# Products that nobody reads in TensorE's waits, and two held low parts moved ahead of expert 0

## The chip, the cores and the metric

The kernel runs on one core of a Trainium2 chip. The metric is the device time of one execution in microseconds (us), the median of several runs; lower is better. In the trace the engines are PE (TensorE's matmuls; PEld are its weight loads), DVE (VectorE), ACT (ScalarE), POOL (GpSimd) and SP (SyncE, which here issues DMAs); a trailing q (SPq, PEq) marks an engine's own queue.

## The reference

One transformer block in float32 on a sequence of 1024 tokens of width 1024: sparse attention and gated linear attention side by side, a layer norm, a hierarchical mixture of 32 experts of which each token takes two, and a second layer norm. What matters for the change is the end:

```python
x = layer_norm(DN_ALPHA * x + gt1[:, None, :] * y, ln1_g[l], ln1_b[l])
h2 = modulate(x, sh2, sc2)
f = hier_moe(h2, w_router_group[l], ..., w_exp_down[l])
x = layer_norm(DN_ALPHA * x + gt2[:, None, :] * f, ln2_g[l], ln2_b[l])
```

In `hier_moe` the router takes the best of 4 groups, then the best 2 of the 8 experts in it; a token's result is the sum of `gate * ((silu(t @ w1) * (t @ w3)) @ w2)` over its two experts.

## The kernel before

Tokens are worked on in eight tiles of 128. float32 products of full precision are made of three fast ones: every operand is split into a high part (ScalarE copies it into the fast format) and a low part (VectorE or GpSimd subtracts the high part from the original), and `mm3` multiplies high by high, high by low and low by high.

**The tiles of the output projection and router.** A loop over tiles computes the output projection (`products`), the residual and first norm, the modulated second norm, the transposes of the tile (`transposed`), the router's products (`logits`, TensorE), the choice of group and experts (`choose`, VectorE), the place of every token among its expert's slots (`place`: two small bf16 products and VectorE work), the list of slots (`slots`, TensorE), the gate weights (`weigh`: VectorE, two exponentials of ScalarE, VectorE) and these weights ordered by slots (`slot_weights`: VectorE masks, TensorE products into `gps`). The last tile, 7, has an order of its own, written out by hand at the end (from L1622 on). Each engine takes its instructions in the order in which the text issues them (`manual_schedule`); an instruction that waits holds up those behind it on its engine.

In that stretch the first two thirds of expert 0's weights are also split (`split(..., hold=True)`): ScalarE makes four high parts, and the four low parts, each one subtraction of 128x1024 on VectorE, are put on a list `held`; `low_parts(n)` issues the next n of them. Before the change all four stand behind the copies of the slot weights (L1650, L1652): one behind each half of expert 0's transposed input (`expert_x`), then two more, then the count of overfull experts (`count_blocks`) and the low parts of expert 1.

**The experts.** A loop over 32 experts gathers each expert's tokens, transposes them (L1669), multiplies by the gate and up weights (`expert_up`, 24 products of 512 columns into `eph`), gates (`expert_act`: ScalarE at L1682, VectorE at L1683), transposes (L1689) and multiplies by the down weights; results are scattered to `dy`. Weights are loaded ahead into a ring of twelve buffers by SP (`fetch_next`).

**The last stage.** Two rows of `dy` per token are loaded, added, multiplied by `gt2`, added to the kept `xa`, normalized and stored. Its order is the string `LAST`: a letter for a step, a digit for the tile. a and b add the two rows (on TensorE, as products with the identity, for tiles 3 and 5, else on VectorE), g multiplies by `gt2` (L1857, VectorE), x and z add `xa` and the gated rows as products with the identity into a buffer `fps` of PSUM, of which there are four (L1851; tiles 0 and 7 do it on VectorE instead), m copies the sum from PSUM with its mean (L1864, ScalarE), v takes the variance (squares on ScalarE at L1870, then a root on GpSimd, L1871 and L1872), s and o scale and shift (L1875, L1882, VectorE), and o stores. x1 to x4 need no rows of `dy` and stand first; the first step of TensorE that needs such rows is z1.

Of the kernel before, what the change touches and what calls it, by code (L numbers as in the profile page):

```python
# [21 lines left out]
D = 1024  # L22
# [59 lines left out]


LAST = """
x1 x2 x3 x4 b0 g0 m0 b1 v0 g1 s0 z1 b2 m1 o0 v1 a3 g2 s1 z2 b4 b3 m2 o1 v2 a5 g4 g3 z4 s2 z3 m4 b6
o2 v4 b5 g6 m3 x5 s4 v3 g5 x6 o4 z5 s3 b7 z6 m5 o3 v5 g7 m6 s5 v6 m7 o5 v7 s6 s7 o6 o7
"""

# [70 lines left out]
def block_kernel(ctx, tc, A, out, dbg=None, stop=99):  # L159
# [1132 lines left out]
    GP.iota(pid, pattern=[[S, 2], [128, NT]], base=1, channel_multiplier=1, allow_small_or_imprecise_dtypes=True)  # L1292
    ones = rtp.tile([128, 128], BF, name="ones")
    GP.memset(ones, 1.0)
    gat = rtp.tile([128, 2, NT], F32, name="gat")
    exf = rtp.tile([128, 2, NT], F32, name="exf")
    psf = rtp.tile([128, 2, NT], F32, name="psf")
# [40 lines left out]
        V.tensor_scalar(M1, iota[:, :NE], exf[:, 0, t:t + 1], None, op0=OP.is_equal)  # L1338
        V.scalar_tensor_tensor(Mb[:, t], iota[:, :NE], exf[:, 1, t:t + 1], M1, op0=OP.is_equal, op1=OP.add)

    def weigh(t):

        L, g8, m8 = (rt[t].pop(n) for n in ("L", "g8", "m8"))
        ng_ = rtw.tile([128, 4], F32, name="rng")
        V.tensor_tensor(ng_[:, 0:1], m8[:, 1:2], m8[:, 0:1], op=OP.subtract)
        V.tensor_tensor(L[:, :4], L[:, :4], g8[:, 0:1].to_broadcast([128, 4]), op=OP.subtract)
        SC.activation(L[:, :4], L[:, :4], AF.Exp, accum_out=ng_[:, 1:2])
        SC.activation(ng_[:, 0:1], ng_[:, 0:1], AF.Exp)
        V.scalar_tensor_tensor(ng_[:, 2:3], ng_[:, 0:1], 1.0, ng_[:, 1:2], op0=OP.add, op1=OP.mult)
        V.reciprocal(gat[:, 0, t:t + 1], ng_[:, 2:3])  # L1350
        V.tensor_tensor(gat[:, 1, t:t + 1], gat[:, 0, t:t + 1], ng_[:, 0:1], op=OP.mult)

    def place(t):

# [202 lines left out]
    def low_parts(n):  # L1557
        for _ in range(min(n, len(held))):
            V.tensor_tensor(*held.pop(0), op=OP.subtract)  # L1559
# [67 lines left out]
    W[0, 0] = split(raws.pop((0, 0)), 0, hold=True)  # L1627
    z = fast_second(t)
    place(t - 2)
    transposed(t)  # L1630
    W[0, 1] = split(raws.pop((0, 1)), 1, hold=True)
    fetch_next(FE1)
# [6 lines left out]
    choose(t)  # L1639
    place(t)  # L1640
    slots(t)
    keep(t, z)
    slot_rows(tps, 0, NE, rtp)
    for i in range(NX):
        gather_x(xg[i], gidx[:, i:i + 1])
    for i in range(2):
        weigh(t - 1 + i)
    for i in range(3):
        slot_weights(t - 2 + i)
    V.tensor_copy(gsl[:, :NE], gps)  # L1650
    PE.matmul(pos[:, NT], ones, run[:, NT], start=True, stop=True, skip_group_check=True)
    V.tensor_copy(cnt, pos[:, NT])  # L1652
# [114 lines left out]
    with tc.tile_pool(name="ex", bufs=2) as ex, tc.tile_pool(name="epp", bufs=1, space=PSUM) as epp:  # L1767
        prev = []
        for X in expert_x(ex, epp, xg[0]):
            low_parts(1)  # L1770
        low_parts(2)
        gather_x(xg[0], gidx[:, NX:NX + 1])
        fetch_next(FE0)
        count_blocks()

        def down(e):
            return expert_down(ex, epp, W.pop((e, 2)), Hs)

        def scatter(y, e):
            sc_ = scatter_y(y, sidx[:, e:e + 1])  # L1780
            for p_ in prev:
                tc.declare_no_dep(sc_.ins, p_.ins, reason="rows of other slots")
            prev.append(sc_)

        for e in range(NE):
            fetch_next(3)
            more = e + 1 < NE
            ph = expert_up(epp, (W.pop((e, 0)), W.pop((e, 1))), X)
            if more:
                for i in range(2):  # L1790
                    W[e + 1, i] = split(raws.pop((e + 1, i)), i)
            sg = expert_act(es2, ph, gsl[:, e:e + 1])
            if more:
                *_, X = expert_x(ex, epp, xg[(e + 1) % NX])
                if e + 1 + NX < NE:
                    gather_x(xg[(e + 1) % NX], gidx[:, e + 1 + NX:e + 2 + NX])
            W[e, 2] = split(raws.pop((e, 2)), 2)
            sc_ = down(e - 1) if e > 0 else None
            Hs = expert_h(es2, epp, sg)
            if e > 0:  # L1800
                scatter(sc_, e - 1)
            if e == NE - 4:
                xa = []
                for _ in range(FX0):
                    load_xa(SY)
                gb, gt2 = (page(pe).rearrange("p (t n) -> p t n", t=2) for _ in range(2))
                for j, src in enumerate(("ln2_g", "ln2_b")):
                    SY.dma_start(gb[:, j], A[src][0:1].to_broadcast([128, D]))
                gt2 = gt2[:, 0]
                SY.dma_start(gt2, dada[3:4].to_broadcast([128, D]))  # L1810
        scatter(down(NE - 1), NE - 1)
# [24 lines left out]
    with tc.tile_pool(name="fin", bufs=NT) as fp, tc.tile_pool(name="fpp", bufs=4, space=PSUM) as fpp:  # L1836
# [5 lines left out]
        fs = {}  # L1842
        st = fp.tile([128, 4, NT], F32, name="fst", bufs=1)
        s_, m_, q_, r_ = (st[:, i] for i in range(4))
        def summed(t, j, x, first):

            if first:
                fs[t, j] = fpp.tile([128, D], F32, name="fps")
            for half in range(2):
                sl = slice(half * 512, half * 512 + 512)  # L1850
                PE.matmul(fs[t, j][:, sl], ident, x[:, sl], start=first, stop=not first)  # L1851

        def added(t):
            V.tensor_tensor(rr[t], rr[t], r2s[t], op=OP.add)
# [22 lines left out]
        def shift(t):  # L1877
# [10 lines left out]
            "g": gated,  # L1888
            "x": lambda t: summed(t, 1, xa[t], True),
            "z": lambda t: summed(t, 1, rr[t], False),  # L1890
            "m": mean, "v": variance, "s": scale, "o": shift,
        }
        with tc.manual_schedule(engines=ALL):
# [32 lines left out]
```

## Time and profile before

| | us |
|---|---|
| median of 3 runs | 1409.38 |
| lowest and highest run | 1406.3 and 1409.62 |
| profiled execution | 1403.06 |
| its span, first to last instruction | 1401.3 |
| TensorE busy | 1308.8 (93%) |
| VectorE busy | 1145.8 (82%) |
| ScalarE busy | 717.4 (51%) |
| GpSimd busy | 440.5 (31%) |
| mean granted clock of TensorE | 0.967 |

Times within the trace count from the first instruction. The span is cut into stages by what runs: projections and attention up to about 875, the tiles of the output projection and router up to about 1030, the experts up to about 1344, the last stage behind that. The granted clock is a share of 2.4 GHz, and the rows show it at one of two levels, 1.0 and 0.5 (1.2 GHz); a mean between them is a stretch with both.

In a row of the timeline stand start, duration, engine, line, operation, output and inputs by the program's names, partitions by elements, how many instructions are merged, and in brackets the idle time of the engine ahead of it with what ended it. The duration of a matmul is modelled and overlaps with the next one; starts of neighbours give the pace.

### The profile page before, as it was taken

The page shows a single profiled execution, that of the slowest core. Times are in us where ns is not written, and L with a number is a line of the kernel's source. Part 1 is how long each engine was busy: PE and PEld are TensorE (multiplying, and loading weights), DVE is VectorE, ACT ScalarE, POOL GpSimd, SP SyncE. Part 2 cuts the span into 40 slices and gives each one's busy share as a digit, 9 for nine tenths or more (in the row PEclk, how much of TensorE's full clock was granted, in tenths as well). Part 3 has the DMA queues.
Part 4 walks back from the last instruction along what each step waited for, and adds up shares of the span by engine and source line. Part 5 has one row for each costly group of instructions (what it writes and reads, how often), then busy time and mean ns, then how long its engine had stood idle before and what let it go on. Part 6 is the DMA issues. An engine that isn't in the chain of part 4 may idle for free. (4 is left out here: it accounts for less than half of the span.)

```text
span 1401.3 us, 21266 instructions
## 1 busy us (share of the span) xinstructions
PE 1308.8 (93%) x7535; PEld 1057.7 (75%) x7535; DVE 1145.8 (82%) x2137; ACT 717.4 (51%) x1306; POOL 440.5 (31%) x474
## 2 busy tenths in 40 slices
PE   4989999999999999998989999999779999999965
PEld 2568888887888788985557778999758888888832
DVE  5738888887988899974788749788889999999947
ACT  1546765444244321323665644222248888889824
POOL 2422123375237521232544425211212222222114
PEclk9999999999999999999999999999869999999987
DMA  8475422112211223103864458745469999999954
GB/s 285 158 210 183 138 78 76 43 56 73 72 61 39 74 87 106 61 31 122 318 230 138 137 152 261 273 168 209 151 214 374 372 381 371 373 348 363 375 224 177
DMA packets 133998, 264.91 MB, mean 189 GB/s; under 512 B 20736, under 2 KB 71224, under 8 KB 131840
## 3 DMA queue, kind: packets, MB, share of 16 engines
q1 hardware_dynamic: 122960, 245.40, 50.4%
q0 software_dynamic: 9216, 16.80, 3.2%
q8 instruction: 60, 0.98, 0.3%
q10 hardware_dynamic: 1712, 1.32, 0.3%
q14 instruction: 50, 0.41, 0.1%
HBM read 229.61 MB, written 50.62 MB: 200 GB/s over the span
## 5 line engine op out<-in xcount | busy, mean ns | idle before, releaser
L1554 DVE TENSOR_TENSOR elo<-pg,ehi 128x1024 fp32r<-128x1024 f32 x188 | 219.0, 1219 | 17.6 <-ACT ehi L1549 8.9
L181 PE MATMUL pj<-hTh,whi 128*128 128x512 f32 (+1 forms) x528 | 211.0, 400 | 0.0
L182 PE MATMUL pj<-hTl,whi 128*128 128x512 f32 (+1 forms) x528 | 207.1, 392 | 1.9 <-DVE hTl L307 1.2
L183 PE MATMUL pj<-hTh,wlo 128*128 128x512 f32 (+1 forms) x528 | 207.2, 392 | 0.1
L815 POOL TENSOR_TENSOR wlo<-raw,whi 128x512 fp32r<-128x512 f32 x84 | 114.5, 1378 | 289.0 <-ACT whi L814 268.8
L1549 ACT ACTIVATE ehi<-pg 128x1024 fp32r<-128x1024 f32 x192 | 190.1, 1075 | 1.0 <-PE eph L183 1.0
L517 DVE MATCH_REPLACE8 acc<-m,acc 128x1024 f32<-128x1024 f32 (+2 forms) x192 | 167.1, 878 | 0.0
L514 DVE MAX8 m<-acc 128x8 f32<-128x1024 f32 (+2 forms) x192 | 162.2, 881 | 0.0
L496 DVE SCALAR_TENSOR_TENSOR acc<-ixr,iwt,acc 128x128 f32<-128x128 f32 (+3 forms) x120 | 107.3, 933 | 23.9 <-ACT ixr L489 23.1
L181 PEld LDWEIGHTS pj<-hTh,whi 128*128 128x128 f32 (+1 forms) x528 | 98.6, 187 | 23.1 <-issue 1.7
L183 PEld LDWEIGHTS pj<-hTh,wlo 128*128 128x128 f32 (+1 forms) x528 | 98.5, 186 | 22.9 <-issue 0.6
L182 PEld LDWEIGHTS pj<-hTl,whi 128*128 128x128 f32 (+1 forms) x528 | 98.8, 187 | 22.2 <-DVE hTl L307 2.7
L181 PE MATMUL pj<-whi,hTh 128*128 128x256 f32 x384 | 111.8, 291 | 0.0
L182 PE MATMUL pj<-wlo,hTh 128*128 128x256 f32 x384 | 108.6, 283 | 0.0
L183 PE MATMUL pj<-whi,hTl 128*128 128x256 f32 x384 | 108.5, 283 | 0.0
L181 PE MATMUL eph<-ehi,xh 128*128 128x512 f32 x256 | 105.4, 412 | 0.0
L182 PE MATMUL eph<-elo,xh 128*128 128x512 f32 x256 | 102.8, 402 | 1.1 <-DVE elo L1559 1.1
L183 PE MATMUL eph<-ehi,xl 128*128 128x512 f32 x256 | 102.4, 400 | 0.0
L489 ACT ACTIVATE ixr<-ips 128x128 f32<-128x128 f32 (+7 forms) x128 | 80.7, 653 | 41.7 <-PE ips L487 32.9
L1573 POOL DMA_INDIRECT xg<-dh,gidx x32 | 34.2, 1070 | 161.4 <-PE etp L1669 139.9
L181 PEld LDWEIGHTS pj<-whi,hTh 128*128 128x128 f32 x384 | 73.4, 191 | 6.9 <-issue 5.5
L181 PE MATMUL yps<-whi,pg 128*128 128x256 f32 x256 | 76.0, 297 | 0.2 <-ACT pg L1234 0.2
(318 smaller groups left out, 3128.2 us busy)
## 6 DMA issues: line engine op xcount, KB each, us to landing
pg<-in_w_exp_gate_dram SPq DMA_DIRECT2D x64, 512.0 KB
pg<-in_w_exp_up_dram SPq DMA_DIRECT2D x64, 512.0 KB
pg<-in_w_exp_down_dram SPq DMA_DIRECT2D x32, 1024.0 KB
raw<-in_w_in_dram SPq DMA_DIRECT2D x20, 1024.0 KB
wada<-in_w_ada_dram SPq DMA_DIRECT2D x16, 1024.0 KB
dgate<-gate SPq DMA_DIRECT2D x48, 256.0 KB
gate<-dgate SPq DMA_DIRECT2D x48, 256.0 KB
wada<-in_w_ada_dram SPq DMA_DIRECT2D x16, 512.0 KB
```

Of the source, the lines that this page charges most:

```text
L181: PE.matmul(ps, ah, bh, start=first, stop=False)
L182: PE.matmul(ps, ah, bl, start=False, stop=False)
L183: PE.matmul(ps, al, bh, start=False, stop=last)
L489: SC.activation(r, ps, AF.Relu)
L496: V.scalar_tensor_tensor(acc[i], r, sc, acc[i], op0=OP.mult, op1=OP.add)
L514: V.max(m, acc[i])
L517: V.match_replace(acc[i], m, acc[i], -3.0e38)
L815: GP.tensor_tensor(lo[:, k:k + 2], raw[:, k:k + 2], hi[:, k:k + 2].bitcast(F32), op=OP.subtract)
L1549: SC.activation(h3, src, AF.Copy)
L1554: V.tensor_tensor(*args, op=OP.subtract)
L1573: GP.indirect_dma_start(out=x, out_offset=None, in_=dh2, in_offset=bass.IndirectOffsetOnAxis(ap=gi, axis=0), bounds_check=S - 1, oob_is_er ...
```

## The change

- A helper `busy(ps, n)` issues n products of the 128x128 bf16 matrix of ones with the same matrix, repeated to 512 columns, into a PSUM tile. Nothing reads the results.
- 20 of them are issued in the last tile behind `place(t - 2)` and ahead of `transposed(t)`, into a further buffer of the ring `yps`.
- 10 of them are issued behind `slots(t)`, ahead of the slot weights.
- In the last stage a new step w4 issues 28 of them between x3 and x4, into tile 4's own buffer `fps`, which x4 then overwrites.
- `weigh` is divided into two parts: up to the exponentials, and the rest. For the last two tiles both first parts are issued, then one held low part, then both second parts.
- Another held low part is issued behind `slot_weights` and ahead of the copy of `gps`. The two that stood behind expert 0's input are gone there.

```diff
@@ -82,7 +82,7 @@
 
 
 LAST = """
-x1 x2 x3 x4 b0 g0 m0 b1 v0 g1 s0 z1 b2 m1 o0 v1 a3 g2 s1 z2 b4 b3 m2 o1 v2 a5 g4 g3 z4 s2 z3 m4 b6
+x1 x2 x3 w4 x4 b0 g0 m0 b1 v0 g1 s0 z1 b2 m1 o0 v1 a3 g2 s1 z2 b4 b3 m2 o1 v2 a5 g4 g3 z4 s2 z3 m4 b6
 o2 v4 b5 g6 m3 x5 s4 v3 g5 x6 o4 z5 s3 b7 z6 m5 o3 v5 g7 m6 s5 v6 m7 o5 v7 s6 s7 o6 o7
 """
 
@@ -1292,6 +1292,11 @@
     GP.iota(pid, pattern=[[S, 2], [128, NT]], base=1, channel_multiplier=1, allow_small_or_imprecise_dtypes=True)
     ones = rtp.tile([128, 128], BF, name="ones")
     GP.memset(ones, 1.0)
+
+    def busy(ps, n):
+
+        for _ in range(n):
+            PE.matmul(ps, ones, ones[:, None, :].to_broadcast([128, 4, 128]), start=True, stop=True)
     gat = rtp.tile([128, 2, NT], F32, name="gat")
     exf = rtp.tile([128, 2, NT], F32, name="exf")
     psf = rtp.tile([128, 2, NT], F32, name="psf")
@@ -1338,17 +1343,20 @@
         V.tensor_scalar(M1, iota[:, :NE], exf[:, 0, t:t + 1], None, op0=OP.is_equal)
         V.scalar_tensor_tensor(Mb[:, t], iota[:, :NE], exf[:, 1, t:t + 1], M1, op0=OP.is_equal, op1=OP.add)
 
-    def weigh(t):
-
-        L, g8, m8 = (rt[t].pop(n) for n in ("L", "g8", "m8"))
-        ng_ = rtw.tile([128, 4], F32, name="rng")
-        V.tensor_tensor(ng_[:, 0:1], m8[:, 1:2], m8[:, 0:1], op=OP.subtract)
-        V.tensor_tensor(L[:, :4], L[:, :4], g8[:, 0:1].to_broadcast([128, 4]), op=OP.subtract)
-        SC.activation(L[:, :4], L[:, :4], AF.Exp, accum_out=ng_[:, 1:2])
-        SC.activation(ng_[:, 0:1], ng_[:, 0:1], AF.Exp)
-        V.scalar_tensor_tensor(ng_[:, 2:3], ng_[:, 0:1], 1.0, ng_[:, 1:2], op0=OP.add, op1=OP.mult)
-        V.reciprocal(gat[:, 0, t:t + 1], ng_[:, 2:3])
-        V.tensor_tensor(gat[:, 1, t:t + 1], gat[:, 0, t:t + 1], ng_[:, 0:1], op=OP.mult)
+    def weigh(t, parts=(0, 1)):
+
+        L, g8, m8 = (rt[t][n] for n in ("L", "g8", "m8"))
+        if 0 in parts:
+            ng_ = rt[t]["ng"] = rtw.tile([128, 4], F32, name="rng")
+            V.tensor_tensor(ng_[:, 0:1], m8[:, 1:2], m8[:, 0:1], op=OP.subtract)
+            V.tensor_tensor(L[:, :4], L[:, :4], g8[:, 0:1].to_broadcast([128, 4]), op=OP.subtract)
+            SC.activation(L[:, :4], L[:, :4], AF.Exp, accum_out=ng_[:, 1:2])
+            SC.activation(ng_[:, 0:1], ng_[:, 0:1], AF.Exp)
+        if 1 in parts:
+            ng_ = rt[t]["ng"]
+            V.scalar_tensor_tensor(ng_[:, 2:3], ng_[:, 0:1], 1.0, ng_[:, 1:2], op0=OP.add, op1=OP.mult)
+            V.reciprocal(gat[:, 0, t:t + 1], ng_[:, 2:3])
+            V.tensor_tensor(gat[:, 1, t:t + 1], gat[:, 0, t:t + 1], ng_[:, 0:1], op=OP.mult)
 
     def place(t):
 
@@ -1627,6 +1635,7 @@
     W[0, 0] = split(raws.pop((0, 0)), 0, hold=True)
     z = fast_second(t)
     place(t - 2)
+    busy(lpp.tile([128, 512], F32, name="yps", bufs=5), 20)
     transposed(t)
     W[0, 1] = split(raws.pop((0, 1)), 1, hold=True)
     fetch_next(FE1)
@@ -1639,14 +1648,19 @@
     choose(t)
     place(t)
     slots(t)
+    busy(lpp.tile([128, 512], F32, name="yps", bufs=5), 10)
     keep(t, z)
     slot_rows(tps, 0, NE, rtp)
     for i in range(NX):
         gather_x(xg[i], gidx[:, i:i + 1])
     for i in range(2):
-        weigh(t - 1 + i)
+        weigh(t - 1 + i, (0,))
+    low_parts(1)
+    for i in range(2):
+        weigh(t - 1 + i, (1,))
     for i in range(3):
         slot_weights(t - 2 + i)
+    low_parts(1)
     V.tensor_copy(gsl[:, :NE], gps)
     PE.matmul(pos[:, NT], ones, run[:, NT], start=True, stop=True, skip_group_check=True)
     V.tensor_copy(cnt, pos[:, NT])
@@ -1768,7 +1782,6 @@
         prev = []
         for X in expert_x(ex, epp, xg[0]):
             low_parts(1)
-        low_parts(2)
         gather_x(xg[0], gidx[:, NX:NX + 1])
         fetch_next(FE0)
         count_blocks()
@@ -1842,13 +1855,18 @@
         fs = {}
         st = fp.tile([128, 4, NT], F32, name="fst", bufs=1)
         s_, m_, q_, r_ = (st[:, i] for i in range(4))
+
+        def tile_of(t, j):
+            if (t, j) not in fs:
+                fs[t, j] = fpp.tile([128, D], F32, name="fps")
+            return fs[t, j]
+
         def summed(t, j, x, first):
 
-            if first:
-                fs[t, j] = fpp.tile([128, D], F32, name="fps")
+            ps = tile_of(t, j)
             for half in range(2):
                 sl = slice(half * 512, half * 512 + 512)
-                PE.matmul(fs[t, j][:, sl], ident, x[:, sl], start=first, stop=not first)
+                PE.matmul(ps[:, sl], ident, x[:, sl], start=first, stop=not first)
 
         def added(t):
             V.tensor_tensor(rr[t], rr[t], r2s[t], op=OP.add)
@@ -1888,6 +1906,7 @@
             "g": gated,
             "x": lambda t: summed(t, 1, xa[t], True),
             "z": lambda t: summed(t, 1, rr[t], False),
+            "w": lambda t: busy(tile_of(t, 1)[:, :512], 28),
             "m": mean, "v": variance, "s": scale, "o": shift,
         }
         with tc.manual_schedule(engines=ALL):
```

## Rows read from the trace of the kernel before

**Rows 1.** Windows of the span, busy time per engine; last columns: granted clock, DMA share, GB/s

```profile
965.00:970.00 5.00, 5.00 (x32) 5.00 (x32) 3.89 (x19) 0.39 (x3) 0.00 (x0) 0.66 0.38 151
...
1007.00:1010.00 3.00, 0.00 (x0) 0.00 (x0) 2.90 (x5) 0.00 (x0) 2.72 (x4) 0.50 0.77 313
...
1260.00:1270.00 10.00, 10.00 (x50) 8.22 (x49) 9.41 (x12) 8.40 (x12) 2.10 (x2) 1.00 0.97 372
...
1360.00:1365.00 5.00, 3.79 (x5) 1.19 (x5) 4.48 (x4) 1.26 (x3) 1.45 (x1) 0.50 1.03 414
```

**Rows 2.** Timeline, end of the last tile: start, duration, engine, line, idle and releaser

```profile
1006.45 0.18 PE L1356 MATMUL sums<-run,ones 128*128 128x32 bf16 x1
...
1012.52 1.94 PE L1519 MATMUL yps<-ident,lx 128*128 128x128 f32 x8 [5.89 <-DVE lx L1507]
...
1018.46 0.20 DVE L1322 TENSOR_TENSOR rL<-yps,br 128x40 f32<-128x40 f32 x1 [0.27 <-PE yps L1528]
```

**Rows 3.** Timeline, slots and slot weights, up to expert 0's first transposes

```profile
1022.33 0.61 PE L1374 MATMUL tps<-rE,rP 128*128 128x32 f32 x2 [0.94 <-DVE rP L1369]
...
1024.51 0.16 DVE L1349 SCALAR_TENSOR_TENSOR rng<-rng 128x1 f32<-128x1 f32 x1 [0.46 <-ACT rng L1348]
...
1026.13 1.34 DVE L1379 TENSOR_SCALAR rEg<-jp,exf,gat 128x32 f32<-128x32 f32 x6
...
1026.48 2.77 PE L1380 MATMUL gps<-rEg,rP 128*128 128x32 f32 x12 [3.54 <-DVE rEg L1379]
...
1029.29 0.19 DVE L1650 COPY gsl<-gps 128x32 f32<-128x32 f32 x1 [1.82 <-PE sums L1651]
...
1029.63 1.97 PE L1669 MATMUL etp<-ident,xg 128*128 128x128 f32 x8 [0.35 <-DVE cnt L1652]
```

**Rows 4.** Timeline, expert 0, VectorE and TensorE

```profile
1031.46 0.69 DVE L1671 TENSOR_TENSOR xl<-etp,xh 128x512 fp32r<-128x512 f32 x1 [1.89 <-ACT xh L1670]
...
1033.34 0.79 PE L182 MATMUL eph<-elo,xh 128*128 128x512 f32 x1 [1.06 <-DVE elo L1559]
...
1033.81 3.49 DVE L1559 TENSOR_TENSOR elo<-pg,ehi 128x1024 fp32r<-128x1024 f32 x3
...
1043.69 0.46 DVE L1683 SCALAR_TENSOR_TENSOR esg<-esg,gsl,eph 128x256 f32<-128x256 f32 x1
...
1044.20 0.44 PE L1689 MATMUL ehp<-ident,esg 128*128 128x128 f32 x2 [2.36 <-DVE esg L1683]
```

**Rows 5.** Timeline, 512-column products of expert 0, two at each clock

```profile
1034.36 0.63 PE L181 MATMUL eph<-ehi,xh 128*128 128x512 f32 x1
...
1037.35 0.58 PE L182 MATMUL eph<-elo,xh 128*128 128x512 f32 x1
...
1038.46 0.40 PE L183 MATMUL eph<-ehi,xl 128*128 128x512 f32 x1
...
1040.56 0.40 PE L183 MATMUL eph<-ehi,xl 128*128 128x512 f32 x1
```

**Rows 6.** Timeline, ScalarE in a later expert

```profile
1061.33 0.39 ACT L1682 ACTIVATE esg<-eph 128x256 f32<-128x256 f32 x1 [1.06 <-PE eph L183]
```

**Rows 7.** Timeline, last stage

```profile
1344.89 7.13 PE L1851 MATMUL fps<-pg,ident 128*128 128x512 f32 x16 [1.17 <-ACTq L1817]
...
1359.92 3.75 PE L1851 MATMUL fps<-fr,ident 128*128 128x512 f32 x4 [7.90 <-POOL fst L1871]
...
1363.71 1.02 ACT L1864 ACTIVATE fr<-fps 128x1024 f32<-128x1024 f32 x1 [4.57 <-PE fps L1851]
...
1366.36 1.28 DVE L1875 SCALAR_TENSOR_TENSOR fr<-fr,fst,pg 128x1024 f32<-128x1024 f32 x1 [1.89 <-ACT fj L1870]
...
1395.12 1.42 DVE L1882 SCALAR_TENSOR_TENSOR fr<-fr,fst,pg 128x512 f32<-128x512 f32 x2 [0.44 <-POOL fst L1872]
```

**Rows 8.** Groups of VectorE in 1352 to 1397: busy, mean ns; idle before, releasers

```profile
L1882 DVE SCALAR_TENSOR_TENSOR fr<-fr,fst,pg 128x1024 f32<-128x1024 f32 (+1 forms) x9 | 10.4, 1161 | 1.3 <-POOL fst L1872 1.3
...
L1875 DVE SCALAR_TENSOR_TENSOR fr<-fr,fst,pg 128x1024 f32<-128x1024 f32 x8 | 10.2, 1280 | 2.4 <-ACT fj L1870 2.4
```

## The prediction

> **What bounds the kernel now.** I began with the windows of the span, whose next-to-last columns are the granted clock and the DMA share. In the long run of experts TensorE is busy 10.00 us of each 10 at the full clock, while the loads hold the DMA engines at 0.97 [rows 1]; ScalarE waits for TensorE's product each time [rows 6]. There TensorE sets the pace, and nothing of the change lies there. Two other places stand at 0.50 of the clock, the lower level of 1.2 GHz instead of 2.4: the end of the last tile with the start of expert 0, and the head of the last stage [rows 1]. In both the clock fell while TensorE was waiting or had only short products.
>
> The timeline then shows who ends each wait. In the last tile it is VectorE: the transposes wait 5.89 us for the second norm [rows 2], the slot weights 3.54 us for the gate weights [rows 3]. VectorE itself is free for pieces of that stretch: 0.46 us ahead of a weight (once for each of two tiles), 1.82 us ahead of the copy of the slot weights, 1.89 us ahead of expert 0's first low part [rows 3, 4]. From then on it is full: it reaches the gating product of expert 0 at 1043.69, and TensorE stands 2.36 us for that [rows 4]. So VectorE, not TensorE, ends the start of the experts. In the last stage products wait 7.90 us for VectorE, then run at half clock (four in 3.75 us), and VectorE next waits 1.89 us for the chain behind them [rows 7].
>
> **The price of a product.** At half clock seven 512-column products start within 1037.35 - 1034.36 = 2.99 us, 0.427 us each; at the full clock nine within 1040.56 - 1038.46 = 2.10 us, 0.233 each [rows 5]. The trace has no bf16 product of 512 columns; its only bf16 ones have 32 [rows 2]. I take 0.233 and 0.427, the nearest in length. The upper end at the full clock is the last stage's float32 form, 7.13 / 16 = 0.446 per instruction [rows 7]. As an estimate, the Trainium skill's page "TensorE: Matmul & The Clock Gate", section "Wait — 56ns, not 53.3ns?", has 215.7 and 426.7 ns for a bf16 product of this length; by it the 28 take 6.0 us where I have 6.5, and the end of the kernel is the same, since both end inside the wait.
>
> **Part 1, 20 products ahead of the last transposes.** They follow the product that ends at 1006.63 and lie under the 5.89 us wait, until 1012.52 [rows 2]. At half clock all the way they end at 1006.63 + 8.5 = 1015.2, 2.7 us late; all at the full clock at 1011.3. In expert 0 it rose between 1037.35 and 1038.46, after dense products from 1033.34 [rows 4, 5]; if it rises as far into the fillers, nine or so cost 0.427 and eleven 0.233: 1006.63 + 3.8 + 2.6 = 1013.0, 0.5 us late. The eight transposes then need some 1.0 us instead of 1.94 [rows 2], so they end where they did. The next choice waits for the router's products only 0.27 us [rows 2]; that is the most to gain. I take -0.2, from -0.3 to +2.7, the lower end being the nearer by the price of rows 5.
>
> **Part 2, 10 products behind the last slots.** They start at 1022.9 [rows 3]. At half clock they end at 1027.2, 0.7 us after the slot weights could start at 1026.48; if the clock rises on the way, about 1026.8. The twelve slot-weight products then take about 1.6 us at the full clock instead of 2.77 [rows 3]: end 1028.8 instead of 1029.25. If it does not rise: 1030.0. I take -0.4, from -0.5 to +0.7.
>
> A rule speaks against both: TensorE's starts stand in program order in every row of the trace here. The Trainium skill, "TensorE: Matmul & The Clock Gate", section "Part 3: Packing small matmuls — row/col tiling", says that matmuls keep strict order, so a filler that outlasts its wait holds up the real product; the trace agrees. By that Parts 1 and 2 would cost up to 2.7 and 0.7; it is the rival C below.
>
> **Part 3, two low parts.** One is worth 3.49 / 3 = 1.16 us of VectorE [rows 4]. The first now stands between the halves of the weights; it fills the two waits of 0.46 us [rows 3] and delays the rest by 1.16 - 0.92 = 0.24. The two activations ahead of it are done before it ends, as both weights' first halves now go first. The second fills the 1.82 us ahead of the copy [rows 3] and costs nothing; without that cover it would cost 1.16. What they leave is VectorE's full stretch from 1031.46 to 1043.69: 12.23 - 2.3 = 9.9 us. Nothing else there falls: ScalarE's high parts of expert 1 lie ahead of their low parts by more than 2.3 us. TensorE no longer waits 1.06 us for a low part [rows 4], and its 24 products, started near 1030.6, end by 1038.6 even with eight at half clock, ahead of the gating product's new time. So VectorE still decides.
>
> Sum for the start of the experts: -2.3 for the low parts, +0.2 (the one's overhang, on the chain to the slot weights), -0.4 (slot weights), -0.2 (last tile): -2.7. Bounds: -1.6 where the clock stays low through the slot weights, -3.1 at best; one half-clock stretch in expert 1 may vanish as well, eight products at 0.427 - 0.233 = -1.6 [rows 5]. From there TensorE is full through all experts, so the shift goes to their end. The loads move too: they wait for buffers that the low parts and products free, so they are asked for earlier by as much.
>
> **Part 4, 28 products in the last stage.** Three of four sums ahead take 12 x 0.446 = 5.3 us from 1344.89; the 28 take 6.5, the fourth sum 1.8: 1358.5 [rows 7]. The waiting product starts at 1359.92 as before, since VectorE releases it; 1.4 us stay idle. At the full clock four instructions take 1.8 instead of 3.75 us, so the copy at 1363.71 comes at 1361.7, and the scaling at 1366.36 starts when its predecessor ends, 1364.5: -1.9. What is late next is VectorE itself, which is busy nearly all of the time from there: it waits 2.4 us in all for ScalarE's squares and 1.3 us for GpSimd's roots [rows 8]. TensorE's stretch behind the first product shortens as well, so the other waits for squares should go (2.4 - 1.89 = 0.5), and those for roots but the last one, of the last tile (1.3 - 0.44 = 0.9) [rows 7, 8], since a root then has its time while VectorE works on other tiles. That is -1.9 - 0.5 - 0.9 = -3.3, and the last shift starts near 1391.8 instead of 1395.12. Bounds: -1.9 (the first wait alone) and -3.7 (all of rows 8); -1.0 if the clock dips once more between the waits and half of the first gain goes. If all the wait were filled to no effect on the clock, 0.
>
> **The sum.** The profiled execution is 1403.06 us. Less 2.7 and 3.3 it is 1397.1. The median shown is 1409.38, 6.3 us above that execution, and the stretches at half clock can fall elsewhere in each execution; the change is taken off the median: 1409.4 - 6.0 = 1403.4. About 0.3%, 4.2 us, is what a measurement can tell from no change.
>
> **Rivals.** *A: the last stage gives nothing*, because VectorE and the arrival of the rows decide it: the DMA share is 1.03 there [rows 1], and VectorE is busy 4.48 of 5 us. Against it stands the 1.89 us wait for TensorE's chain. Time: 1409.4 - 2.7 = 1406.7. *B: the experts give nothing back*, because the loads (share 0.97, [rows 1]) become the bound and the earlier start is paid out as waits. Against it: ScalarE never waits for a load there. Time: 1409.4 - 3.3 = 1406.1. *C, slower: the fillers overrun.* If bf16 products of this form go at 0.427 us throughout, Part 1 costs 2.7, Part 2 0.7, and the 28 take 12 us, so the waiting product starts at 1364.0 instead of 1359.92 (+4.1, less 1.9 for its own full clock: +2.2); low parts -2.3: 1409.4 + 3.3 = 1412.7. It decides from a price of 0.28 us a product in the last stage, where 28 fill the 7.90 us wait. *D: the change does not hold the clock.* The clock did fall to a mean of 0.66 in a stretch where TensorE was busy 5.00 of 5 us [rows 1], so being busy alone does not hold it. Then the low parts alone pay, less the overruns: 1409.4 - 2.3 + 0.9 = 1408.0.
>
> **How the numbers follow.** Forecast 0.60 (1403.4, from 1399 with all best ends to 1406), A 0.17, B 0.09, C 0.06, D 0.08. The range takes the best ends (-3.1 - 1.6 - 3.7 = -8.4: 1401.0, and 3 us more for a median as low as the lowest of the runs shown: 1398) and A and B, to 1407.6: 0.06 and 0.08 stay out. Faster by over 0.3% means under 1405.2: nearly all of the forecast and a little of A and B: 0.62; within: 0.31; slower: 0.07.
>
> **What would show it.** Right: the gating product of expert 0 about 2.7 us sooner after the last tile's norm, with two low parts ahead of the copy of the slot weights; the transposes and the slot weights at the full clock; the first released product of the last stage in about 1.8 us and VectorE's wait of 1.89 us gone. Wrong: a slot-weight product that waits behind fillers, a clock still at 0.50 after them, a product of 512 columns well over 0.233 us, a new wait of ScalarE for a load in the experts, or a last stage as long as before from its first product to its end.

## The result

| | before | after |
|---|---|---|
| median, us | 1403.35 (20 runs) | 1396.26 (20 runs) |
| lowest and highest | 1395.07 and 1409.62 | 1389.45 and 1401.41 |
| profiled execution | 1403.06 | 1396.65 |

The ratio is 0.9950 with a 95% interval of 0.9933 to 0.9967: the change takes 7.0 us off (4.6 to 9.4). The forecast change of 6.0 us lies inside that interval, but it was taken from another start: the median of the kernel before is 1403.35 over 20 runs, not the 1409.38 of the first three, and so the time of the changed kernel lies 1.7 us below the range that was given.

A line of the profile's page shows the granted clock in 40 slices of the span, in tenths; first the kernel before, then the changed one. Slices 29, 30, 39 and 40 have gained a tenth each; slices 19 and 27, which lie ahead of the change, stand at 8 now.

```profile
PEclk9999999999999999999999999999869999999987
```

```profile
PEclk9999999999999999998999999989979999999998
```

The timeline of the changed kernel from the last tile's second scaling to the gating product of expert 0, with the columns of [rows 2]:

```profile
1008.97 1.31 DVE L1512 SCALAR_TENSOR_TENSOR lx<-lx,x2m,rowsc 128x1024 f32<-128x1024 f32 x1
...
1005.57 4.48 PE L1299 MATMUL yps<-ones 128*128 128x512 bf16 x20
...
1011.63 1.29 PE L1527 MATMUL yps<-ident,lx 128*128 128x128 f32 x8 [1.58 <-DVE lx L1515]
...
1016.00 0.19 PE L1363 MATMUL sums<-Mb,upper 128*128 128x32 bf16 x1 [1.41 <-DVE Mb L1344]
...
1016.05 1.48 PE L1536 MATMUL yps<-wr,lhT 128*128 128x40 f32 x6
...
1017.57 0.20 DVE L1327 TENSOR_TENSOR rL<-yps,br 128x40 f32<-128x40 f32 x1 [0.27 <-PE yps L1536]
...
1021.90 4.16 PE L1299 MATMUL yps<-ones 128*128 128x512 bf16 x10
...
1023.24 1.22 DVE L1567 TENSOR_TENSOR elo<-pg,ehi 128x1024 fp32r<-128x1024 f32 x1
...
1023.26 2.40 POOL L1581 DMA_INDIRECT xg<-dh,gidx  x1 [12.56 <-DVE rL L1352]
...
1025.89 1.42 PE L1388 MATMUL gps<-rEg,rP 128*128 128x32 f32 x12
...
1027.68 0.18 DVE L1664 COPY gsl<-gps 128x32 f32<-128x32 f32 x1
...
1029.01 1.95 PE L1683 MATMUL etp<-ident,xg 128*128 128x128 f32 x8 [1.69 <-DMA xg<-dh,gidx]
...
1030.82 0.69 DVE L1685 TENSOR_TENSOR xl<-etp,xh 128x512 fp32r<-128x512 f32 x1 [2.86 <-ACT xh L1684]
...
1040.78 0.46 DVE L1697 SCALAR_TENSOR_TENSOR esg<-esg,gsl,eph 128x256 f32<-128x256 f32 x1
```

Two windows of the same trace, with the granted clock in the third column from the end:

```profile
1015.00:1020.00 5.00, 2.35 (x12) 2.29 (x12) 4.24 (x27) 1.55 (x2) 0.00 (x0) 0.54 0.26 105
1020.00:1025.00 5.00, 3.77 (x12) 1.74 (x12) 4.28 (x24) 0.67 (x6) 1.74 (x1) 0.50 0.00 2
```

The 20 products run at the full clock, end near 1010.0 and leave 1.58 us of the 5.89 us wait of [rows 2]; the transposes behind them take 1.29 us instead of 1.94. But the last six router products stand behind `place` of tile 6, which waits 1.41 us for VectorE's mask, so they start as late as before, 7.1 us after the second scaling. They take 1.48 us again, since the granted clock has fallen to the lower level (0.54 from 1015 to 1020), and the next choice still waits 0.27 us, as in [rows 2]. The 10 products take 4 us, nearly all at the lower level (0.50 from 1020 to 1025); the clock is at 1.00 again for the twelve slot-weight products, which take 1.42 us instead of 2.77. The copy of the slot weights comes 18.71 us after the second scaling, 19.42 before (there from 1009.87 to 1029.29 [rows 3]). Then a wait stands that was not there: the transposes of expert 0 wait 1.69 us for the first gather, whose instruction on GpSimd took 2.40 us. From the second scaling to the gating product it is 31.81 us instead of 33.82.

One row of a later expert on ScalarE answers to [rows 6]; the loop's wait and pace are what they were.

```profile
1058.41 0.39 ACT L1696 ACTIVATE esg<-eph 128x256 f32<-128x256 f32 x1 [1.05 <-PE eph L183]
```

The last stage, where the row with x28 is step w4:

```profile
1341.98 5.42 PE L1869 MATMUL fps<-pg,ident 128*128 128x512 f32 x12 [1.18 <-ACTq L1830]
...
1347.24 6.21 PE L1299 MATMUL fps<-ones 128*128 128x512 bf16 x28
...
1356.71 1.96 PE L1869 MATMUL fps<-fr,ident 128*128 128x512 f32 x4 [1.55 <-POOL fst L1889]
...
1358.70 1.02 ACT L1882 ACTIVATE fr<-fps 128x1024 f32<-128x1024 f32 x1 [2.77 <-PE fps L1869]
...
1361.36 1.28 DVE L1893 SCALAR_TENSOR_TENSOR fr<-fr,fst,pg 128x1024 f32<-128x1024 f32 x1
...
1388.71 1.41 DVE L1900 SCALAR_TENSOR_TENSOR fr<-fr,fst,pg 128x512 f32<-128x512 f32 x2 [0.44 <-POOL fst L1890]
```

The first product that waits stands 1.55 us idle instead of 7.90 [rows 7], its four instructions take 1.96 us instead of 3.75, the copy comes 16.7 us after the first product instead of 18.8, and the last shift 46.73 us after it instead of 50.23. VectorE's groups in that stage answer to [rows 8]:

```profile
L1900 DVE SCALAR_TENSOR_TENSOR fr<-fr,fst,pg 128x1024 f32<-128x1024 f32 (+1 forms) x9 | 10.4, 1161 | 1.3 <-POOL fst L1890 1.3
...
L1893 DVE SCALAR_TENSOR_TENSOR fr<-fr,fst,pg 128x1024 f32<-128x1024 f32 x8 | 10.1, 1278 | 0.1
```

The wait for ScalarE's squares is down from 2.4 to 0.1 us; that for GpSimd's roots is 1.3 us, as before.

### The profile page after: what moved, and what is told of

Read it like the earlier page. It is cut to its first block, busy times and chain, and to the rows that moved or that the text cites. A ratio compares the mean times of both kernels' runs of the same rounds, so it can differ in the third digit from the quotient of the medians.

```text
span 1394.8 us, 21381 instructions
## 1 busy us (share of the span) xinstructions
PE 1312.3 (94%) x7593; PEld 1056.8 (76%) x7593; DVE 1145.4 (82%) x2137; ACT 717.6 (51%) x1306; POOL 441.3 (32%) x474
## 3 DMA queue, kind: packets, MB, share of 16 engines
q1 hardware_dynamic: 122960, 245.40, 50.3%
```

## The experiments

The stages were read from one trace each, in us; the first column runs from the second scaling of the last tile to expert 0's gating product on VectorE (L1683 before), the second from there to expert 1's activation on ScalarE (L1682), the third from the first product of the last stage to the start of the last shift. The kernels differ in what the change moves, not in the stages ahead of the first column. What lies between the columns does not differ either: from expert 1's activation to that of the last expert all 14 traces have 285.1 us, from there to the last stage 8.0, and from the start of the last shift to the end of the trace 6.1.

| kernel | start of experts | expert 1 | last stage | ratio to before (95%) |
|---|---|---|---|---|
| before | 33.82 | 8.13 | 50.23 | |
| before, again | 33.82 | 8.14 | 50.03 | 1.0007 (0.9990 to 1.0025) |
| after | 31.81 | 8.13 | 46.73 | 0.9950 (0.9933 to 0.9967) |
| after, again | 31.25 | 6.59 | 46.92 | 0.9935 (0.9910 to 0.9960) |
| w4 alone | 33.80 | 8.14 | 46.96 | 0.9994 (0.9980 to 1.0009) |
| w4 alone, again | 33.85 | 6.60 | 47.03 | 0.9979 (0.9957 to 1.0001) |
| low parts alone | 31.86 | 6.61 | 50.34 | 0.9974 (0.9961 to 0.9988) |
| 20 and 10 alone | 32.68 | 8.78 | 50.42 | 1.0004 (0.9984 to 1.0024) |
| after without 20 and 10 | 32.02 | 6.60 | 47.37 | 0.9951 (0.9931 to 0.9971) |
| after with 8 in w4 | 31.16 | 6.60 | 50.58 | one run, 1397.1 us |
| after with 56 in w4 | 31.25 | 6.60 | 50.98 | 0.9972 (0.9955 to 0.9988) |
| low parts later | 30.65 | 7.92 | 46.90 | 0.9967 (0.9951 to 0.9983) |
| three low parts later | 29.09 | 6.60 | 47.11 | 0.9950 (0.9926 to 0.9974) |
| the same without 20 and 10 | 30.04 | 6.59 | 48.79 | 0.9937 (0.9912 to 0.9962) |

**The kernel before, once more.** Nothing is edited.

> The kernel before, unchanged, profiled once more. If the spread of its times (1395 to 1410 us) comes from where the half-clock stretches fall, its trace should differ from the first one by under 1 us wherever the clock was the same, and by one stretch (about 1.6 us for eight products of 512 columns) where it was not; times a ratio of 1.000. If the spread comes from the loads instead, stages with DMA shares near 1 should differ by several us at the same clock.

Its profiled span is 1405.3 us, 4.0 more than the first. All three stages of the table repeat within 0.2 us; the second scaling starts at 1014.11 instead of 1009.87. The two windows below are the projection tiles ahead of the change, first of this trace, then of the run with the low parts alone, whose code is the same up to there and whose second scaling starts at 1005.91:

```profile
880.00:1005.00 125.00, 120.22 (x931) 118.41 (x930) 98.18 (x250) 30.06 (x72) 22.03 (x35) 0.92 0.55 195
```

```profile
880.00:1005.00 125.00, 116.89 (x955) 115.04 (x955) 102.18 (x261) 31.54 (x76) 25.22 (x39) 0.97 0.59 208
```

The granted clock is 0.92 in the one and 0.97 in the other at nearly the same DMA share. A share of 0.05 of 125 us is 6.2 us of full clock, of the 8.2 us between them; from the same instruction of VectorE ahead of these tiles (the gate product at 864.13 in the one, 861.82 in the other) to the second scaling the two differ by 5.9 us. So most of what lies between this pair is where the half-clock stretches fall ahead of the change, and by its size that can account for most of the spread between runs of one kernel; run by run it was not followed, and what makes the stretches fall differently was not tried.

**The 28 products alone.**

```diff
-x1 x2 x3 x4 b0 g0 m0
+x1 x2 x3 w4 x4 b0 g0 m0
```

> Only the 28 products of the last stage. Theory (they keep the clock, VectorE's waits go): from the first product of the last stage to the start of the last shift 46.7 us instead of 50.2, experts as before; time -3.3 us, ratio 0.9976. Rival (the row loads and VectorE set that stage, and the 0.3 us earlier rows of the changed kernel are all): 50 us, ratio 1.000.

The timeline of its last stage:

```profile
1346.18 5.42 PE L1864 MATMUL fps<-pg,ident 128*128 128x512 f32 x12 [1.17 <-ACTq L1825]
...
1361.14 1.96 PE L1864 MATMUL fps<-fr,ident 128*128 128x512 f32 x4 [1.78 <-POOL fst L1884]
...
1393.14 1.41 DVE L1895 SCALAR_TENSOR_TENSOR fr<-fr,fst,pg 128x512 f32<-128x512 f32 x2 [0.44 <-POOL fst L1885]
```

The stage is 46.96 us, 3.3 less, all of the theory's gain, in the stage where the rows arrive no sooner than before (first VectorE sum 8.71 us after the first product, 8.77 before). The time, however, moved by -0.8 us with an interval of -2.8 to +1.3. The same kernel was measured once more:

> Only the 28 products of the last stage, once more, since the first time -0.8 us (interval -2.8 to +1.3) was measured where its trace had 3.3 us. Theory (the trace is right, the rest was the spread of the stages ahead of it): 46.9 us again for the last stage and a ratio of 0.9977. Rival (something outside that stage gives 2 us back): 46.9 us, and 0.9994 again.

The stage is 47.03 us and the time -2.9 us (-6.0 to +0.1). The trace's gain lies inside this interval and half a microsecond outside the first. These times alone exclude neither that part of the gain is given back nor that there is none. In the two traces nothing is given back: every stage from the second scaling to the end is as in the kernel before, to 0.03 us, or shorter.

**The two low parts alone.** The change without all three groups of unread products.

```diff
     for i in range(2):
-        weigh(t - 1 + i)
+        weigh(t - 1 + i, (0,))
+    low_parts(1)
+    for i in range(2):
+        weigh(t - 1 + i, (1,))
     for i in range(3):
         slot_weights(t - 2 + i)
+    low_parts(1)
...
         for X in expert_x(ex, epp, xg[0]):
             low_parts(1)
-        low_parts(2)
```

> Only the two low parts and the divided weights, no unread products. Theory (VectorE ends the start of the experts, so the low parts pay alone): gating product of expert 0 about 2.0 us sooner after the last tile's second scaling than in the kernel before (33.82 us there, 31.81 in the changed kernel), ratio 0.9986. Rival (without the clock TensorE's 24 products end later than VectorE): 0 to 1 us sooner. The first gather's instruction on GpSimd should take about 2.4 us instead of 1.3 if VectorE's low part beside it delays it.

```profile
1020.19 2.40 POOL L1581 DMA_INDIRECT xg<-dh,gidx  x1 [12.56 <-DVE rL L1352]
...
1025.43 0.19 DVE L1662 COPY gsl<-gps 128x32 f32<-128x32 f32 x1 [0.74 <-PE sums L1663]
...
1026.02 1.95 PE L1681 MATMUL etp<-ident,xg 128*128 128x128 f32 x8 [0.60 <-DMA xg<-dh,gidx]
...
1037.77 0.46 DVE L1695 SCALAR_TENSOR_TENSOR esg<-esg,gsl,eph 128x256 f32<-128x256 f32 x1
```

The gating product comes 31.86 us after the second scaling, 1.96 sooner, without any help of the clock: VectorE ends the start of the experts. The copy comes a little later than before (19.52 us for 19.42), as the first low part's overhang says. The gather's instruction takes 2.40 us here too. The time is 3.6 us below the kernel before (1.7 to 5.5), where 2.0 was expected; in this trace expert 1 has no half-clock stretch (6.61 us for 8.13), a further 1.5 us.

**The 20 and the 10 alone.** The kernel before with these two groups:

```diff
     place(t - 2)
+    busy(lpp.tile([128, 512], F32, name="yps", bufs=5), 20)
     transposed(t)
...
     slots(t)
+    busy(lpp.tile([128, 512], F32, name="yps", bufs=5), 10)
     keep(t, z)
```

> Only the 20 and the 10 products ahead of the experts. Theory (VectorE is the bound there): the copy of the slot weights comes 0.4 to 0.7 us sooner after the last tile's second scaling, the gating product of expert 0 between 0.2 and 0.7 us sooner; time within 0.7 us, ratio 0.9995. Rival (the clock alone carries the gain of the start): about 2 us sooner. The first gather's instruction should stay at 1.3 us, since no low part stands beside it.

```profile
1029.13 1.31 POOL L1581 DMA_INDIRECT xg<-dh,gidx  x1 [12.33 <-DVE rL L1352]
...
1033.78 0.19 DVE L1660 COPY gsl<-gps 128x32 f32<-128x32 f32 x1 [1.31 <-PE sums L1661]
...
1034.12 1.16 PE L1679 MATMUL etp<-ident,xg 128*128 128x128 f32 x8 [0.37 <-DVE cnt L1662]
...
1047.76 0.46 DVE L1693 SCALAR_TENSOR_TENSOR esg<-esg,gsl,eph 128x256 f32<-128x256 f32 x1
```

The copy comes 18.70 us after the second scaling (-0.7) and the gating product 32.68 (-1.1), more than the theory's 0.2 to 0.7 and less than the rival's 2. The gather's instruction is 1.31 us. In expert 1 over half of that is lost again (8.78 us): more products ran at half clock there. The time shows nothing (+0.6 us, -2.2 to +3.4).

**The changed kernel without the 20 and the 10.**

```diff
-    busy(lpp.tile([128, 512], F32, name="yps", bufs=5), 20)
...
-    busy(lpp.tile([128, 512], F32, name="yps", bufs=5), 10)
```

> The changed kernel without the 20 and the 10 products ahead of the experts. Theory (they pay nothing at the end): second scaling of the last tile to the gating product of expert 0 31.9 us (31.81 with them), last stage 46.8 us from its first product to the last shift; time -6.7 us against the kernel before, ratio 0.9952, level with the changed kernel. Rival (they carry part of the gain): 33 us or more, and a time 2 us above the changed kernel's.

32.02 us and 47.37 us; the time is 1396.49 us, -6.9 us (-9.7 to -4.1). Next to the low parts the two groups are worth about half a microsecond: the four traces that have them with the low parts (the changed kernel twice, 8 and 56 in w4) have 31.81, 31.25, 31.16 and 31.25, mean 31.37, against 31.86 and 32.02 without. No time here can tell that from nothing. In the last three of the four the first transposes of expert 0 run at the full clock (1.12 to 1.14 us), in the first at half (1.95 us), which is the half microsecond between these traces.

**8 products in w4 instead of 28.**

```diff
-busy(tile_of(t, 1)[:, :512], 28)
+busy(tile_of(t, 1)[:, :512], 8)
```

> The changed kernel with 8 products instead of 28 in step w4, so that TensorE is idle again for some 6 us ahead of the first product that waits. Theory (the clock is what the 28 buy): that product's four instructions take 3.75 us again instead of 1.96, and the last stage 50 us from its first product to the last shift. Rival (the order alone, x4 behind x3 with a gap, or the earlier rows): 1.96 us and 46.7 us as with 28.

```profile
1343.82 1.89 PE L1299 MATMUL fps<-ones 128*128 128x512 bf16 x8
...
1353.67 3.75 PE L1869 MATMUL fps<-fr,ident 128*128 128x512 f32 x4 [6.24 <-POOL fst L1889]
```

TensorE is idle 6.24 us, the clock falls, the four instructions take 3.75 us and the stage 50.58. The order of the steps is the same as with 28, so what the 28 buy is the clock, not the order.

**56 products in w4.**

```diff
-busy(tile_of(t, 1)[:, :512], 28)
+busy(tile_of(t, 1)[:, :512], 56)
```

> The changed kernel with 56 products in step w4, which take 12.4 us and so outlast the wait: the product that waits starts 19.7 us after the first of the stage instead of 14.7. Theory (TensorE takes them in order, and VectorE has no slack left): last stage 51 to 51.7 us instead of 46.7, worse than before the change (50.2); time about -0.5 to -1.5 us against the kernel before. Rival (an overrun is absorbed, as the loads of the rows go on meanwhile): 47 to 48.5 us.

```profile
1345.61 12.25 PE L1299 MATMUL fps<-ones 128*128 128x512 bf16 x56
...
1359.41 1.88 PE L1869 MATMUL fps<-fr,ident 128*128 128x512 f32 x4
```

The product that waited has no idle time ahead of it now and starts 19.05 us after the first of the stage instead of 14.73. VectorE's group of scalings waits for it:

```profile
L1893 DVE SCALAR_TENSOR_TENSOR fr<-fr,fst,pg 128x1024 f32<-128x1024 f32 x8 | 10.1, 1279 | 4.4 <-ACT fj L1888 4.4
```

That is 4.4 us of waits for 0.1; the stage takes 50.98 us, more than with no filler. A filler that outlasts its wait costs nearly what it lasts too long: 4.3 us at the waiting product, 4.0 in the stage against the mean of 47.0 with 28. The time, though, is 3.9 us below the kernel before (1.7 to 6.3), more than the 0.5 to 1.5 expected: the start of the experts and expert 1 (31.25 and 6.60 us) gave 4.1 us in this trace.

**The low parts away from the gather.** The changed kernel with its two low parts later.

```diff
     for i in range(2):
         weigh(t - 1 + i, (0,))
-    low_parts(1)
     for i in range(2):
         weigh(t - 1 + i, (1,))
     for i in range(3):
         slot_weights(t - 2 + i)
     low_parts(1)
     V.tensor_copy(gsl[:, :NE], gps)
...
     V.tensor_copy(cnt, pos[:, NT])
+    low_parts(1)
```

> The changed kernel with its two low parts moved: the first behind the masks of the slot weights, the second behind the copies, so that none stands beside the first gather's instruction on GpSimd. Theory (the low part beside it made that instruction 2.40 us instead of 1.31, and the gather is what the first transposes wait for): 1.31 us again, second scaling to expert 0's first low part of the input 20.8 us instead of 21.85, to its gating product 30.7 us instead of 31.8. Rival (the gather's landing does not depend on it): 1.31 or 2.4 us, but 21.8 and 31.8 us as before.

```profile
1009.12 6.66 PE L1299 MATMUL yps<-ones 128*128 128x512 bf16 x20
...
1015.61 1.04 PE L1527 MATMUL yps<-ident,lx 128*128 128x128 f32 x8
...
1024.75 1.31 POOL L1581 DMA_INDIRECT xg<-dh,gidx  x1 [12.85 <-DVE rL L1352]
...
1029.48 1.13 PE L1683 MATMUL etp<-ident,xg 128*128 128x128 f32 x8 [0.61 <-DMA xg<-dh,gidx]
...
1030.88 0.69 DVE L1685 TENSOR_TENSOR xl<-etp,xh 128x512 fp32r<-128x512 f32 x1 [0.57 <-ACT xh L1684]
...
1040.83 0.46 DVE L1697 SCALAR_TENSOR_TENSOR esg<-esg,gsl,eph 128x256 f32<-128x256 f32 x1
```

The gather's instruction is 1.31 us again, the wait of the transposes for it 0.61 instead of 1.69, the input's first low part comes 20.70 us after the second scaling instead of 21.85, the gating product 30.65 instead of 31.81, as the theory had them. So the low part beside it did lengthen the gather, and the gather was what the start waited for. But part of the 1.16 us is the clock: the transposes took 1.13 us here and 1.95 in the changed kernel's first trace. Against its second trace, where they took 1.12, the input's first low part comes 0.59 us sooner (21.29 there) and the gating product 0.60 (31.25). The time, 4.6 us below the kernel before (2.4 to 6.9), does not show a gain over the changed kernel.

This trace also shows the overrun that Part 1 of the prediction had as its upper bound: the clock was still low when the 20 products began, they took 6.66 us instead of 4.48, and the transposes of the last tile began 5.43 us after the second scaling instead of 2.66. Part of that went into the wait for VectorE's mask, which is gone, and the products behind ran at the full clock, so the next choice came only 0.3 us later than in the kernel before (8.90 for 8.59).

**Three low parts behind the weights.** The kernel of the run before with one more:

```diff
     V.tensor_copy(cnt, pos[:, NT])
-    low_parts(1)
+    low_parts(2)
```

> As the run before, with a third low part behind the copies, in the 2.86 us that VectorE still waits there in the changed kernel. Theory: three low parts are hidden ahead of the input's first low part; second scaling to the gating product 30.1 us instead of 31.8, time 1.7 us below the changed kernel, ratio to the kernel before 0.994. Rival (the third delays the input's low parts by as much as it saves): 30.7 us as with two.

```profile
1004.61 6.59 PE L1299 MATMUL yps<-ones 128*128 128x512 bf16 x20
...
1024.55 0.19 DVE L1663 COPY gsl<-gps 128x32 f32<-128x32 f32 x1
...
1024.76 2.35 DVE L1567 TENSOR_TENSOR elo<-pg,ehi 128x1024 fp32r<-128x1024 f32 x2
...
1035.90 0.46 DVE L1697 SCALAR_TENSOR_TENSOR esg<-esg,gsl,eph 128x256 f32<-128x256 f32 x1
```

29.09 us, 2.7 below the changed kernel's first trace, 2.2 below its second and 1.56 below the run before. Of the 1.56, 1.14 lie between the input's first low part and the gating product (8.81 us for 9.95): that is the third low part, for the two behind the copies end as the input's high part does and delay nothing. The other 0.42 lie ahead of it, where the choice came 8.23 us after the second scaling instead of 8.90: the 20 overran here too, by 1.6 us (6.59 in all), and the products behind them ran at the full clock. The time, 7.0 us below the kernel before (3.6 to 10.4), is level with the changed kernel's, where 1.7 less was expected.

**The same without the 20 and the 10.**

```diff
-    busy(lpp.tile([128, 512], F32, name="yps", bufs=5), 20)
...
-    busy(lpp.tile([128, 512], F32, name="yps", bufs=5), 10)
```

> The version with three low parts off the first gather, without the 20 and 10 products. Theory (with the gather out of the way the copy of the slot weights is what the start waits for, and the 10 products make it sooner): second scaling to the gating product 30.7 us instead of 29.1 with them. Rival (they pay nothing here either): 29.1 us.

```profile
1025.92 0.19 DVE L1661 COPY gsl<-gps 128x32 f32<-128x32 f32 x1 [0.69 <-PE sums L1662]
...
1037.21 0.46 DVE L1695 SCALAR_TENSOR_TENSOR esg<-esg,gsl,eph 128x256 f32<-128x256 f32 x1
...
1352.08 3.56 PE L1867 MATMUL fps<-fr,ident 128*128 128x512 f32 x4 [2.01 <-POOL fst L1887]
```

30.04 us: with the gather out of the way the copy decides, it comes 18.75 us after the second scaling instead of 17.74, and the unread products are worth 1.0 us between these two traces, between the theory's 1.6 and the rival's 0. It is not the same in every trace: with two low parts in that place, where the 20 overran by 2.8 us, the copy came at 18.71 us, no sooner than the 18.75 here. Its last stage shows something else: with all 28 products and 2.01 us of idle time behind the fourth sum, the four instructions took 3.56 us, and the stage 48.79. The clock dipped there all the same. By its time this kernel (0.9937) is level with the others; the stages say that three low parts with the fillers have the shortest start of the experts, 2.2 to 2.7 us below the changed kernel's, in one trace, and no time here confirms or denies it.

**The changed kernel, once more.** Nothing is edited. Expected were 31.8 us and 46.7 us again, a ratio near 0.996, and an expert 1 with or without the half-clock stretch. It has 31.25, 46.92 and 6.59 us, and 0.9935 (0.9910 to 0.9960).

## Why the prediction was right and wrong

**The step that failed is the sum's last one, by its starting term.** "the change is taken off the median: 1409.4 - 6.0 = 1403.4." The median of three runs was taken for the level of a kernel that spreads over 14.6 us; over 20 runs that term measured 1403.35, 6.0 us less. From there the same sum gives 1397.4, and the range shifts to 1392.0 to 1401.6, with the measured 1396.26 inside. The change itself, forecast at 6.0 us, measured 7.0 (4.6 to 9.4). Both ends of the range stood on that median. (For the best case the text has two values, 1399 in the forecast and 1401.0 in the range; its terms add up to 1401.0. The upper end, 1407.6, lies 0.9 above rival A, and how it was reached is not given.) The two traces compared above show how three runs could lie so high: the projection tiles ahead of the change alone differ by 5.9 us with the clock.

The profiled execution stood in the same text, 6.3 us below the median. From its 1403.06 the sum gave 1397.1; the changed kernel's profiled execution is 1396.65. That this pair fits to half a microsecond is in part luck: 0.9 us of its 6.4 lie ahead of the second scaling, where the change does nothing, and the three stages of the table give 2.0, 0.0 and 3.5 us, 5.5 in all.

**Part 1 (20 products), -0.2: from -0.4 to +0.3.** In the changed kernel's two traces they fit (0.22 us each at the full clock), but the wait of 0.27 us that they should have shortened is unchanged: the last six router products stand behind a wait of 1.41 us for VectorE, so they start no sooner, and the clock fell ahead of them. The trace with 56 in w4 has the same. In two traces (the 20 and 10 alone, 8 in w4) it fell later, and the choice came 0.2 us sooner, as forecast. In two (low parts later, three low parts) they began at half clock and overran by 2.8 and 1.6 us; the choice came 0.3 later in the one and 0.4 sooner in the other. The bound of +2.7 took the overrun for a loss in full; the wait for VectorE's mask took part of it, and the products behind it, at the full clock, made up most or all of the rest.

**Part 2 (10 products), -0.4: -0.7 at the copy in the first trace, and little of it kept.** The copy's gain became a wait for the gather, 1.69 us. The prediction named no such wait: the gather's landing was hidden in the kernel before behind the copies, and no step asked how far.

**Part 3 (low parts), -2.1 with the overhang: -1.9 (31.94 as the mean of the two kernels with them and without the early fillers, against 33.82).** The size is right and one thing in it is missing: the first low part stands beside the gather on GpSimd and lengthens it by 1.1 us. Moving it gave 0.6 us more against the trace with the transposes at the same clock, 1.2 against the other.

**Part 4 (28 products), -3.3: -3.3.** Five traces without 28 to 56 of them have 50.03 to 50.58 us, mean 50.3; of eight with 28, seven have 46.73 to 47.37, mean 47.0, and one, with the dip foretold as "-1.0 if the clock dips once more", 48.79. Of its terms the wait for squares went as said (2.4 to 0.1); the wait for roots stayed at 1.3, where 0.9 was to go; in its place a wait of VectorE of 0.6 us for TensorE's sum of tile 3 went, which was not listed, and the rows came 0.3 us sooner. So one term was mis-sized, by 0.9, two were not listed, and that the sum came out at 3.3 is luck.

**Expert 1's half-clock stretch** ("may vanish as well, -1.6") comes and goes: 8.1 us with it, 6.6 without, and both occur in one kernel (w4 alone twice: 8.14 and 6.60; the changed kernel twice: 8.13 and 6.59). Seven of the nine traces with low parts moved are without it, one of the five others. Whether the change makes it rarer these traces are too few to say.

**The rivals.** A falls by the last stage of the traces with 28, B by the pace of the experts (285.1 us from expert 1 to 31 in all). C's price of 0.28 us a product was not reached in the last stage: 28 start within 1353.28 - 1347.24 = 6.04 us, 0.216 each, a little below the 0.233 that was used. The 215.7 ns that the prediction cites from the Trainium skill, "TensorE: Matmul & The Clock Gate", section "Wait — 56ns, not 53.3ns?", agree with that. The run with 56 and the overrun of the 20 in two traces show the mechanism of C. D holds in part: in the last stage the clock stayed up in seven of eight traces with 28, but ahead of the experts it is back at 0.50 by the last slots in each of the seven traces with the 20.

## What to carry to other kernels

Unread products paid here where three things came together: without them the clock falls in TensorE's idle time, the products behind it end a wait of the bounding engine, and the fillers end before that wait does. The same fillers ahead of work that does not set the end bought about half a microsecond with the low parts, and up to 1.1 us in a trace without them. Work moved into an idle stretch of one engine can slow what another engine does beside it: ask what runs there on GpSimd before putting a long VectorE instruction next to it. Take a predicted change off the level of many runs, not off the median of three; a single traced execution is no level either (1403.06 and 1407.12 us for the kernel before).

## What the hardware showed that was not expected

A gather's instruction on GpSimd took 1.31 us in the kernel before and 2.40 us when a VectorE subtraction of two SBUF tensors (1.22 us) started 0.02 us ahead of it: nearly the subtraction's length more, in each of the six traces with this order (2.40 or 2.41), and 1.31 in each of the others. The third gather beside the second subtraction took 1.36 to 1.74 instead of 0.99. The Trainium skill, "SBUF — State Buffer", section "Who interferes with whom", says that a VectorE instruction with two SBUF inputs contends with a GpSimd instruction that reads SBUF, through a shared read port. The traces agree with that for the indirect gather; which of its reads is held up, they do not show.

The second thing is the dip in the last stage of one trace (three low parts without the 20 and 10). TensorE's idle time behind the dense products does not explain it: it was 2.01 us there, and in the trace of the changed kernel without the 20 and 10 it was 2.19 us and the clock stayed up:

```profile
1357.85 1.96 PE L1867 MATMUL fps<-fr,ident 128*128 128x512 f32 x4 [2.19 <-POOL fst L1887]
```

So 28 fillers did not keep the clock every time; what made the difference these traces do not show.
